# Layer norm's inverse deviation: from a column of sums and a trip through DRAM to products with a constant square

## The chip, the cores and the metric

The kernel runs on one NeuronCore of a Trainium2 chip. The metric is the device time of one execution in microseconds (us). TensorE (PE) multiplies matrices and writes to PSUM, which has 8 banks of 128 x 512 numbers of 4 bytes here. VectorE (DVE) and ScalarE (ACT) work elementwise on SBUF and PSUM, GpSimd (POOL) here mostly issues transfers that add, and SyncE (SP) issues the other transfers. Each engine works off its own list of instructions in order, and the engines wait for each other through semaphores. PEld is the loading of weights into TensorE's array, which overlaps with its products.

## The reference

One decoder layer on x of 1024 tokens by 1024 channels, in float32. The part that the change touches is the layer norm of the conv group, over the 1024 channels of each token:

```python
u = h @ w_in[l]
cv, cg, cs, lx, ls = jnp.split(u, [...], axis=-1)
v = cv * jax.nn.sigmoid(cg)
v = causal_depthwise_conv(v, dw_w[l], dw_b[l])        # 31 taps
v = jax.nn.silu(layernorm(v, cln_g[l], cln_b[l]))
v = v @ pw2_w[l] + pw2_b[l]
y_conv = v * jax.nn.silu(cs)
...
y = jnp.concatenate([y_conv, y_lru], axis=-1) @ w_out[l]
x = x + (1.0 + gate[:, None, :]) * y

def layernorm(x, g, b):
    mu = jnp.mean(xf, axis=-1, keepdims=True)
    var = jnp.mean(jnp.square(xf - mu), axis=-1, keepdims=True)
    y = (xf - mu) * lax.rsqrt(var + EPS)
```

## The kernel before

Channels lie on the partitions and tokens along the free axis: a matrix of 1024 channels by 1024 tokens is KT = 8 tiles of 128 x 1024, and a half (H) is 512 tokens. To keep float32 accuracy, each operand of a product is split into a high and a low part in fp32r (a cast on ScalarE, a subtraction on VectorE), and a product is three: high by high, high by low, low by high. `weights` loads a row of weights as raw, and makes whi (ScalarE, L336) and wlo (VectorE, L363) from it; `mm_k` (L494) emits the three products of 128 x 512 for one tile of the contraction. A row of output takes 8 x 3 products for each half, 48 in all. Their result is called ps, one bank for each half (ps_0, ps_1).

The stages follow each other on TensorE: the products with W_in, the gates of the recurrence, then the 8 rows of the lru half of W_out (m = 0 to 7, operands yh and yl, in the slots ("lru", m)), then the pointwise projection pw2 and the conv half of W_out, both in pairs of rows with seven products in place of eight (`quarters`, `pair_weights`, `pair_products`, L605: results pa, pb, pu, pc). For each lru row VectorE adds the result to x (acc, a SCALAR_TENSOR_TENSOR, L355), and acc goes to DRAM.

Layer norm lies beside the lru rows. `conv_sum` adds the eight tiles c of the convolution into csum; `layer_norm` splits csum into meanh and meanl and multiplies both by a constant square of 1/1024 (ones_r), so that each token's mean stands on every partition (L1262). VectorE subtracts it from each c, ScalarE squares, and VectorE sums the squares over the eight tiles into lnss (128 x 1024). What remains is a sum over the 128 partitions, then the root, then the reciprocal spread to all partitions. `spread_by_dma` does that: eight products with lnss as weights and one column of ones as the moving operand give the sums as a column, 128 tokens on the partitions by 8 (L1234, in plain float32); ScalarE takes the root with eps_t as bias, VectorE the reciprocal, a product with the identity turns it to 8 x 128 (L1238), ScalarE copies that into a piece of V, one transfer writes it to DRAM (lnrowd), and a second reads it back to all 128 partitions (lnbc). VectorE multiplies every c by lnbc, ScalarE applies Silu with the channel's gain and bias, and `quarters` makes the operands of pw2 from c: vha, vla, vhb, vlb, vhc, vlc, vhT, vlT.

The order of the instructions is set by a planner (`Plan`). Each operation has an engine, an estimated cost, a priority (lower goes first), and the buffers that it reads and writes. `Plan.order` runs through time: whenever an engine is free it takes, among the operations whose operands are ready and whose buffers fit in their pools, the one with the lowest priority; an activation whose table isn't loaded counts 2.0 more. Priority −1 in the steps of the root puts them ahead of nearly all else that is ready. What comes out is a fixed list for each engine; on the chip only the semaphores decide when an entry starts.

Of the kernel before, what the change touches and what calls it, by code (L numbers as in the profile page):

```python
# [9 lines left out]
F32 = mybir.dt.float32  # L10
F32R = mybir.dt.float32r
AF = mybir.ActivationFunctionType
ALU = mybir.AluOpType

P = 128
D = 1024
T = 1024
KT = D // P
H = 512
TAPS = 31  # L20
STAPS = 4
EPS = 1e-6
# [5 lines left out]
DWW = SCW + KT * STAPS  # L28
# [59 lines left out]
LOADS = "s0 a0 w0 s1 b0 w1 x1 W2 s2 x2 s3 x3 W4 s4 x4 s5 x5 W6 s6 x6 s7 x7 h0 h1 h2 h3 h4 h5 h6 h7".split()  # L88

SETS = {AF.Sigmoid: "sigmoid", AF.Silu: "silu", AF.Exp: "exp", AF.Tanh: "exp",  # L90
        AF.Sqrt: "sqrt"}


class Buf:
# [199 lines left out]
def hymba_layer(ctx: ExitStack, tc: tile.TileContext, xT, vecs, mod_w, w_first, w_in,  # L294
# [3 lines left out]
    act, dve, pool, pe, sp = nc.scalar, nc.vector, nc.gpsimd, nc.tensor, nc.sync  # L298

    const = ctx.enter_context(tc.tile_pool(name="const", bufs=1))  # L300
# [5 lines left out]
    dram = ctx.enter_context(tc.tile_pool(name="dram", bufs=1, space=bass.MemoryType.DRAM))  # L306
# [11 lines left out]
    S = Plan(pools)  # L318
# [11 lines left out]
    def ACT(prio, out, in_, func, n=T, bias=None, scale=None, accum=None, r=(), w=(),  # L330
            reserve=0, after=()):
        kw = {}

        def emit():
            if func == "copy":
                act.copy(out(), in_())  # L336
                return
            if bias is not None:
                kw["bias"] = bias
            if scale is not None:  # L340
                kw["scale"] = scale
            if accum is not None:
                kw["accum_out"] = accum
            act.activation(out=out(), in_=in_(), func=func, **kw)  # L344
        ptr = sum(x is not None and not isinstance(x, float) for x in (bias, scale))
        return S.op("ACT", a_cost(n, ptr) + (0.1 if accum is not None else 0), emit, prio, r, w,
                    table=SETS.get(func), reserve=reserve, after=after)
# [5 lines left out]
    def STT(prio, out, in0, scalar, in1, op0, op1, n=T, accum=None, r=(), w=(), after=()):  # L353
        def emit():
            dve.scalar_tensor_tensor(out=out(), in0=in0(), scalar=scalar, in1=in1(), op0=op0,  # L355
                                     op1=op1, accum_out=accum)
        return S.op("DVE", d_cost(n, not isinstance(scalar, float)), emit, prio, r, w,
                    lock=not in_psum(r), after=after)

    def TT(prio, eng, out, a, b, op, n=T, r=(), w=(), reserve=0, after=()):  # L360
        e = dve if eng == "DVE" else pool
        return S.op(eng, d_cost(n) if eng == "DVE" else p_cost(n),
                    lambda: e.tensor_tensor(out=out(), in0=a(), in1=b(), op=op), prio, r, w,  # L363
                    reserve=reserve, lock=not in_psum(r), after=after)
# [6 lines left out]
    def SUB(prio, eng, lo, full, hi, n=T, r=(), w=(), reserve=0):  # L371
        return TT(prio, eng, lo, full, lambda: hi().bitcast(F32), ALU.subtract, n, r, w, reserve)
# [8 lines left out]
    def DMA(prio, out, in_, nbytes, r=(), w=(), after=(), reserve=0):  # L381
        return S.op("SP", max(0.1, nbytes / 360e3),
                    lambda: sp.dma_start(out(), in_()), prio, r, w, after=after,
                    reserve=reserve)
# [7 lines left out]
    def big_buf(name, dt=F32, parts=1):  # L392
        return S.buf("big", name, dt, parts)

    def bank(name):
        return S.buf("bank", name)
# [5 lines left out]
    def part(b, a, e):  # L402
        if isinstance(b, Two):
            z = a // H
            return part(b.b[z], a - z * H, e - z * H)
        return lambda: b()[:, a:e]

    def halves(b, a, e):
        if isinstance(b, Two):
            return [(b.b[z], 0) for z in (0, 1) if z * H < e and a < z * H + H]  # L410
        return [(b, i) for i in range(b.parts) if i * (T // b.parts) < e
                and a < (i + 1) * (T // b.parts)]

    FULL_BYTES = P * T * 4


    V = const.tile([P, NVEC], F32, tag="V", name="V")
# [6 lines left out]
    ident = const.tile([P, P], F32, tag="ident", name="ident")  # L424
    make_identity(nc, ident)
    ones = const.tile([P, P], F32, tag="ones", name="ones")
    dve.memset(ones, 1.0)
    ones_r = const.tile([P, P], F32R, tag="ones_r", name="ones_r")
    dve.tensor_scalar(out=ones_r, in0=ones, scalar1=1.0 / D, scalar2=None, op0=ALU.mult)
    eps_t = const.tile([P, 1], F32, tag="eps", name="eps_t")  # L430
    dve.memset(eps_t, EPS)

# [73 lines left out]
    FULL = ((0, H), (H, T))  # L506
# [280 lines left out]
    for i, ld in enumerate(LOADS):  # L787
        p = due[ld] = i - 100.0
# [5 lines left out]
        elif ld[0] in "wW":  # L794
            nk = 1 + (ld[0] == "W")
            rw, hi, lo = fw[k - k % 2]
            n, o, js = nk * FW, (k % 2) * FW, range(k % 2, k % 2 + nk)
            keys = lambda b: [(b, j) for j in js]
            DMA(p, part(rw, o, o + n), lambda k=k, n=nk: w_first[:, k:k + n, :], n * P * 4,
                w=keys(rw))  # L800
            for j in range(k, k + nk):
# [4 lines left out]
                if j:  # L806
                    SUB(p, "DVE", fw_part(lo, j), fw_part(rw, j), fw_part(hi, j), FW,
                        r=[(rw, jj), (hi, jj)], w=[(lo, jj)])
# [35 lines left out]
    for k in range(KT):  # L844
        p = due[f"s{k}"]
# [3 lines left out]
        else:  # L849
            dot(SCALE[k], p - 1.5 * (k == 1), KT + k, [gs_op, *(split_u[:1] if k == 1 else [])])  # L850
        gs_op = S.op("DVE", 0.2, lambda k=k, a_=a_: dve.scalar_tensor_tensor(
            out=col(gs, k), in0=a_, scalar=col(b1, k), in1=vec("norm_g", k), op0=ALU.add,
            op1=ALU.mult), p, [("macc", KT + k), ("b1", 0)], [("gs", k)], lock=True)
        p = max(p, due[f"x{k}"] if k else p, due[f"w{k}"])
# [4 lines left out]
        for a, e in START if k < UK else ((0, T),):  # L859
            n = e - a  # L860
            hk = halves(x_, a, e)
            if k == 0 == a:
                o = TS(p, part(uh, a, e), part(x_, a, e), g, None, ALU.mult, n=n,
                       r=hk + [("gs", k)], w=halves(uh, a, e))
            else:
                o = ACT(p, part(uh, a, e), part(x_, a, e), AF.Copy, n, scale=g,
                        r=hk + [("gs", k)], w=halves(uh, a, e))
            if k == 0 == a:
                rw, hi, lo = fw[0]
                SUB(p, "DVE", fw_part(lo, 0), fw_part(rw, 0), fw_part(hi, 0), FW,  # L870
                    r=[(rw, 0), (hi, 0), *halves(uh, a, e)], w=[(lo, 0)])
# [3 lines left out]
                r=hk + halves(uh, a, e) + [("gs", k)], w=halves(ul, a, e)))  # L875
# [9 lines left out]
        for ch, (a, e) in enumerate(START):  # L885
            for i, ps in enumerate(psf):
                if (a, e) not in cuts[i] or k == 0 == a:
                    continue
                q = p + 0.1 * ch if k < LASTK else due[f"w{KT - 1}"] + 0.01 * ((i + 1) % 4) + 0.001 * ch
# [140 lines left out]
    v, c = {}, {}  # L1030
# [194 lines left out]
               w=[("gate1", i) for i in range(KT)])  # L1225


    def spread_by_dma(ss):
        pr, ps = -1, bank("lnss")
        sd, rs = S.buf("sd", "lnsd"), S.buf("rs", "lnrs")  # L1230

        def stats():
            for b in range(KT):
                pe.matmul(part(ps, b, b + 1)(), ss()[:, b * P:b * P + P], ones[:, 0:1],  # L1234
                          start=b == 0, stop=b == KT - 1, skip_group_check=True)

        def turn():
            pe.matmul(ps()[:KT, P:2 * P], rs()[:, :KT], ident, start=True, stop=True)  # L1238
        S.op("PE", 0.23 * KT, stats, pr, [ss], [ps], columns=4 * P * KT)
        ACT(pr, lambda: sd()[:, :KT], part(ps, 0, KT), AF.Sqrt, KT, bias=eps_t, scale=1.0 / D,  # L1240
            r=[ps], w=[sd])
        S.op("DVE", 0.2, lambda: dve.reciprocal(rs()[:, :KT], sd()[:, :KT]), pr, [sd], [rs])
        S.op("PE", 0.2, turn, pr, [rs], [ps], columns=4 * P)
        row, bc = V[:KT, DWW:DWW + P], big_buf("lnbc", parts=2)
        flat = dram.tile([KT, P], F32, tag="lnrow", name="lnrowd")
        ACT(pr, lambda: row, lambda: ps()[:KT, P:2 * P], "copy", P, r=[ps], w=[("V", 1)])
        DMA(pr, lambda: flat, lambda: row, KT * P * 4, r=[("V", 1)], w=[("lnrowd", 0)])
        DMA(pr, bc, lambda: flat.rearrange("b p -> (b p)").partition_broadcast(P), FULL_BYTES,
            r=[("lnrowd", 0)], w=[bc])
        return bc  # L1250

    def layer_norm():
        pr = 45
        mean = Two("mean")

        mh, ml = big_buf("meanh", F32R), big_buf("meanl", F32R)
        split(-1, mh, ml, csum)

        def mean_mm():
            for a, b in FULL:  # L1260
                for z, m in enumerate((mh, ml)):
                    pe.matmul(part(mean, a, b)(), ones_r, m()[:, a:b], start=z == 0, stop=z == 1)  # L1262
        S.op("PE", 0.91, mean_mm, -1, [mh, ml], mean.b)
        ss = big_buf("lnss")
        for t in range(KT):
            for a, b in FULL:
                TT(pr, "DVE", part(c[t], a, b), part(c[t], a, b), part(mean, a, b), ALU.subtract,
                   H, r=halves(c[t], a, b) + halves(mean, a, b), w=halves(c[t], a, b))
            if t == 0:
                ACT(pr, ss, c[t], AF.Square, r=[c[t]], w=[ss])  # L1270
            else:
                q = big_buf(f"lnsq{t}")
                ACT(pr, q, c[t], AF.Square, r=[c[t]], w=[q])
                TT(pr, "DVE", ss, ss, q, ALU.add, r=[ss, q], w=[ss])
        bc = spread_by_dma(ss)
        for t in range(KT):
            for a, b in FULL:
                TT(pr, "DVE", part(c[t], a, b), part(c[t], a, b), part(bc, a, b), ALU.mult, H,
                   r=halves(c[t], a, b) + halves(bc, a, b), w=halves(c[t], a, b))
            ACT(pr, c[t], c[t], AF.Silu, scale=vec("cln_g", t), bias=vec("cln_b", t), r=[c[t]],  # L1280
                w=[c[t]])

# [285 lines left out]
```

## Time and profile before

| | us |
|---|---|
| median of 3 runs (735.17 to 735.5) | 735.18 |
| the profiled execution | 735.33 |
| its span, from the first to the last instruction | 733.0 |
| PE busy | 723.8 (99%) |
| PEld busy | 601.9 (82%) |
| DVE busy | 636.8 (87%) |
| ACT busy | 458.6 (63%) |
| POOL busy | 98.0 (13%) |

The mean TensorE clock granted was 0.998. Times in the profile count from the start of the span; 2.33 us of the execution lie outside of it. A row of the list of instructions in time has the start, the duration, the engine, the line, the operation, result <- operands, the partitions x elements of both, and the count; in brackets stands the idle time of the engine just before and what ended it. A row of the chain has start, length, engine, result and line. In the list of waits the three numbers are the total, the count and the longest. Ends of products are modelled, so their starts are the better measure.

### The profile page before, as it was taken

The page shows a single profiled execution, that of the slowest core. Times are in us where ns is not written, and L with a number is a line of the kernel's source. Part 1 is how long each engine was busy: PE and PEld are TensorE (multiplying, and loading weights), DVE is VectorE, ACT ScalarE, POOL GpSimd, SP SyncE. Part 2 cuts the span into 40 slices and gives each one's busy share as a digit, 9 for nine tenths or more (in the row PEclk, how much of TensorE's full clock was granted, in tenths as well). Part 3 has the DMA queues.
Part 4 walks back from the last instruction along what each step waited for, and adds up shares of the span by engine and source line. Part 5 has one row for each costly group of instructions (what it writes and reads, how often), then busy time and mean ns, then how long its engine had stood idle before and what let it go on. Part 6 is the DMA issues. An engine that isn't in the chain of part 4 may idle for free.

```text
span 733.0 us, 8975 instructions
## 1 busy us (share of the span) xinstructions
PE 723.8 (99%) x3298; PEld 601.9 (82%) x3298; DVE 636.8 (87%) x907; ACT 458.6 (63%) x616; POOL 98.0 (13%) x107
## 2 busy tenths in 40 slices
PE   8999999999999999999999999999999999999996
PEld 7888888888888888888888888888888888887886
DVE  6999999899999987688899995997699757899647
ACT  6760585776877977957867896834564324656421
POOL 0034012031222332233121100000000000000001
PEclk9999999999999999999999999999999999999999
DMA  9952023388699699699884536343433430622306
GB/s 327 406 210 87 0 82 86 99 199 187 145 251 242 137 214 232 138 220 205 187 175 89 118 82 186 104 155 144 143 116 128 159 116 1 228 76 98 115 1 229
DMA packets 37498, 112.10 MB, mean 153 GB/s; under 512 B 4168, under 2 KB 12880, under 8 KB 37456
## 3 DMA queue, kind: packets, MB, share of 16 engines
q1 hardware_dynamic: 24064, 76.50, 29.4%
q0 software_dynamic: 12528, 34.26, 26.1%
q10 hardware_dynamic: 864, 0.79, 0.3%
q8 instruction: 25, 0.41, 0.2%
q14 instruction: 17, 0.14, 0.1%
HBM read 64.69 MB, written 12.59 MB: 105 GB/s over the span
## 4 chain that ended last, share of the span: by engine, by line
PE 96%; DVE 2%; DMA 1%; SPq 0%; ACT 0%; issue 0%; DVEq 0%
PE ps L494 65%; PE first L774 5%; PE pbpw L605 3%; PE pupw L605 3%; PE papw L605 3%; PE gate L1197 3%; PE puout L605 2%; PE paout L605 2%; PE out L675 2%; PE pcpw L605 1%; PE pb0out L605 1%; PE pcout L605 1%; DVE o L355 1%; DMA fraw<-in_w_first_dram 1%; PE late L774 1%; PE out6b L675 1%
## 5 line engine op out<-in xcount | busy, mean ns | idle before, releaser
L494 PE MATMUL ps<-uh,whi 128*128 128x512 f32 x576 | 224.2, 389 | 0.0
L494 PE MATMUL ps<-ul,whi 128*128 128x512 f32 x576 | 224.1, 389 | 0.0
L494 PE MATMUL ps<-uh,wlo 128*128 128x512 f32 x576 | 224.1, 389 | 0.0
L494 PEld LDWEIGHTS ps<-ul,whi 128*128 128x128 f32 x576 | 108.1, 188 | 22.5
L494 PEld LDWEIGHTS ps<-uh,whi 128*128 128x128 f32 x576 | 108.1, 188 | 22.5
L494 PEld LDWEIGHTS ps<-uh,wlo 128*128 128x128 f32 x576 | 108.1, 188 | 22.4
L336 ACT CAST whi<-raw 128x1024 fp32r<-128x1024 f32 x46 | 48.0, 1048 | 48.6 <-PE ps L494 39.0
L344 ACT ACT_TABLE_LOAD x48 | 61.6, 1283 | 6.2 <-DVE sp8h L377 3.1
L368 POOL DMA_DIRECT2D es<-cq x45 | 40.1, 904 | 164.5 <-ACT cq L344 130.1
L363 DVE TENSOR_TENSOR wlo<-raw,whi 128x1024 fp32r<-128x1024 f32 x39 | 47.5, 1219 | 14.8 <-ACT whi L336 14.5
L355 DVE SCALAR_TENSOR_TENSOR cacc<-v,V,cacc 128x511 f32<-128x511 f32 (+14 forms) x75 | 55.6, 741 | 0.5
L355 DVE SCALAR_TENSOR_TENSOR caccs<-v,V,caccs 128x511 f32<-128x511 f32 (+6 forms) x70 | 52.1, 744 | 1.3
L355 DVE SCALAR_TENSOR_TENSOR caccs<-c,wsum,caccs 128x511 f32<-128x511 f32 (+6 forms) x70 | 51.9, 742 | 0.5
L368 POOL DMA_DIRECT2D oo<-co x42 | 38.3, 913 | 89.3 <-ACT co L344 48.5
L494 PE MATMUL ps<-yh,whi 128*128 128x512 f32 x128 | 50.0, 391 | 0.0
L494 PE MATMUL ps<-yh,wlo 128*128 128x512 f32 x128 | 49.8, 389 | 0.0
L494 PE MATMUL ps<-yl,whi 128*128 128x512 f32 x128 | 49.8, 389 | 0.0
L363 POOL TENSOR_TENSOR o<-fin,bc 128x256 f32<-128x256 f32 x4 | 2.9, 730 | 284.1 <-DMA out_dram<-o 279.0
L355 DVE SCALAR_TENSOR_TENSOR xs<-ps,V,xs 128x512 f32<-128x512 f32 (+3 forms) x48 | 35.7, 744 | 0.2
L344 ACT ACTIVATE cq<-v,V 128x511 f32<-128x511 f32 (+14 forms) x45 | 31.9, 708 | 0.0
L355 DVE SCALAR_TENSOR_TENSOR modw<-modw,sc 128x1024 f32<-128x1024 f32 x23 | 30.1, 1312 | 0.0
L344 ACT ACTIVATE cq<-c,wsum 128x512 f32<-128x512 f32 x42 | 29.9, 714 | 0.0
(375 smaller groups left out, 1443.1 us busy)
## 6 DMA issues: line engine op xcount, KB each, us to landing
raw<-in_w_in_dram SPq DMA_DIRECT2D x36, 512.0 KB, 4.4
modw<-in_mod_w_dram SPq DMA_DIRECT2D x24, 512.0 KB, 9.0
raw<-in_w_out_dram SPq DMA_DIRECT2D x10, 512.0 KB, 3.8
scsd<-scs SPq DMA_DIRECT2D x8, 512.0 KB, 4.7
acc<-in_xT_dram SPq DMA_DIRECT2D x8, 512.0 KB, 4.4
accd<-acc SPq DMA_DIRECT2D x8, 512.0 KB, 2.7
rawpw<-in_pw_dram SPq DMA_DIRECT2D x8, 512.0 KB, 3.5
scsr<-scsd SPq DMA_DIRECT2D x8, 512.0 KB, 5.5
```

Source lines behind the costliest of these rows:

```text
L336: act.copy(out(), in_())
L344: act.activation(out=out(), in_=in_(), func=func, **kw)
L355: dve.scalar_tensor_tensor(out=out(), in0=in0(), scalar=scalar, in1=in1(), op0=op0, op1=op1, accum_out=accum)
L363: lambda: e.tensor_tensor(out=out(), in0=a(), in1=b(), op=op), prio, r, w,
L368: return S.op("POOL", ISSUE, lambda: pool.dma_start(out(), a(), accum_op=ALU.add), prio, r, w, lag=RATE * n / T, after=after)
L494: pe.matmul(part(ps, a - off, b - off)(), k3(lhs)()[:, k, :], rhs[k]()[:, a:b], start=(k == 0 and lhs is wh and rhs is xh and (a - off) % ...
L605: pe.matmul(part(ps, 0, c1 - c0)(), half(*lhs)()[:, j * P:j * P + P], half(*rhs)()[:, c0:c1], start=start and j == 0 and z == 0, stop=j == ...
L675: pe.matmul(part(ps, a - off, e - off)(), k3(lhs)()[:, k, :], rhs()[:, i * H + a % H:i * H + a % H + e - a], start=k == KORD[0] and lhs is ...
L774: pe.matmul(part(ps, a - off, b - off)(), fw_part(lhs, k, i * P, i * P + P)(), rhs()[:, a:b], start=k == 0 and lhs is wh and rhs is xh, st ...
L1197: pe.matmul(ps(), lhs()[:, j, :], rhs()[:, c0:c1], start=st == 0, stop=st == 2)
```

## The change

The trip through DRAM goes. In its place `root_by_ones` treats each half of 512 tokens by itself: ScalarE casts the half of lnss to fp32r (hi), VectorE subtracts to get lo, and TensorE multiplies both by a constant square, so that the sum over the partitions comes out on every partition at once. The square is now −1/1024 (minus_r, also used for the mean, whose subtraction becomes an addition); the bank holds minus the variance. ScalarE takes Abs_reciprocal_sqrt of it with scale −1 and bias eps_t, which gives a first y, and half its square (q). Two SCALAR_TENSOR_TENSORs on VectorE make one step of Newton's method, y · (1.5 − (var + eps) · y² / 2), into lnbc of that half. The multiplications of c then read the half's own lnbc.

```diff
-        AF.Sqrt: "sqrt"}
+        AF.Sqrt: "sqrt", AF.Abs_reciprocal_sqrt: "root"}
...
-    dve.tensor_scalar(out=ones_r, in0=ones, scalar1=1.0 / D, scalar2=None, op0=ALU.mult)
+    dve.tensor_scalar(out=minus_r, in0=ones, scalar1=-1.0 / D, scalar2=None, op0=ALU.mult)
...
-    def spread_by_dma(ss):
...
+    def root_by_ones(pr, ss, a, e, ps, out):
+        n, y, name = e - a, part(out, 0, e - a), f"{ss.name}{a}"
+        hi, lo, q = (big_buf(f"{z}{name}", d) for z, d in (("hi", F32R), ("lo", F32R), ("q", F32)))
+        neg, sk = part(ps, 0, n), halves(ss, a, e)
+        ACT(pr, part(hi, 0, n), part(ss, a, e), "copy", n, r=sk, w=[hi])
+        SUB(pr, "DVE", part(lo, 0, n), part(ss, a, e), part(hi, 0, n), n, r=[*sk, hi], w=[lo])
+
+        def total():
+            for i, m in enumerate((hi, lo)):
+                pe.matmul(neg(), minus_r, part(m, 0, n)(), start=i == 0, stop=i == 1)
+        S.op("PE", 2 * (n + 32) / 2400, total, pr, [hi, lo], [ps], columns=2 * n)
+        ACT(pr, y, neg, AF.Abs_reciprocal_sqrt, n, bias=eps_t, scale=-1.0, r=[ps], w=[out])
+        ACT(pr, part(q, 0, n), y, AF.Square, n, scale=0.5 ** 0.5, r=[out], w=[q])
+        STT(pr, neg, neg, -EPS, part(q, 0, n), ALU.add, ALU.mult, n, r=[ps, q], w=[ps])
+        STT(pr, y, neg, 1.5, y, ALU.add, ALU.mult, n, r=[ps, out], w=[out])
...
-                    pe.matmul(part(mean, a, b)(), ones_r, m()[:, a:b], start=z == 0, stop=z == 1)
+                    pe.matmul(part(mean, a, b)(), minus_r, m()[:, a:b], start=z == 0, stop=z == 1)
...
-        ss = big_buf("lnss")
+        ss = big_buf("lnss", parts=2)
...
-                TT(pr, "DVE", part(c[t], a, b), part(c[t], a, b), part(mean, a, b), ALU.subtract,
+                TT(pr, "DVE", part(c[t], a, b), part(c[t], a, b), part(mean, a, b), ALU.add,
...
-        bc = spread_by_dma(ss)
+        bc = [big_buf(f"lnbc{z}") for z in (0, 1)]
+        for z, (a, b) in enumerate(FULL):
+            root_by_ones(-1, ss, a, b, bank(f"lnss{z}"), bc[z])
         for t in range(KT):
-            for a, b in FULL:
-                TT(pr, "DVE", part(c[t], a, b), part(c[t], a, b), part(bc, a, b), ALU.mult, H,
-                   r=halves(c[t], a, b) + halves(bc, a, b), w=halves(c[t], a, b))
+            for z, (a, b) in enumerate(FULL):
+                TT(pr, "DVE", part(c[t], a, b), part(c[t], a, b), part(bc[z], 0, H), ALU.mult, H,
+                   r=halves(c[t], a, b) + [bc[z]], w=halves(c[t], a, b))
```

Since the planner works out the whole list anew, the diff doesn't show where things stand. The lists differ only from the sums of squares to the start of pw2; ahead of that and from the end of pw2's first pair on, every engine's order is the same. In the names below, numbers tell buffers of one name apart.

TensorE before, where the sums stand among the products of lru row 3, first half; the turn follows 12 products later:

```order
L494 MATMUL ps_0_4151<-yh_3883,whi_4076 128x512
L494 MATMUL ps_0_4151<-yl_3900,whi_4076 128x512
L494 MATMUL ps_0_4151<-yh_3883,wlo_4090 128x512
L1234 MATMUL lnss<-ones,lnss 128x1 x8
L494 MATMUL ps_0_4151<-yh_3893,whi_4076 128x512
L494 MATMUL ps_0_4151<-yl_3911,whi_4076 128x512
```

TensorE now, at the same row of W_out:

```order
L494 MATMUL ps_0_4150<-yh_3892,wlo_4089 128x512
L494 MATMUL ps_0_4150<-yh_3897,whi_4075 128x512
L494 MATMUL ps_0_4150<-yl_3922,whi_4075 128x512
L494 MATMUL ps_0_4150<-yh_3897,wlo_4089 128x512
L1237 MATMUL lnss_4188<-hilnss_4172,minus_r 128x512
L1237 MATMUL lnss_4188<-lolnss_4179,minus_r 128x512
L1237 MATMUL lnss_4191<-hilnss_4174,minus_r 128x512
L1237 MATMUL lnss_4191<-lolnss_4186,minus_r 128x512
L494 MATMUL ps_0_4150<-yh_3908,whi_4075 128x512
```

The four new products stand six main products later than the sums did, and six main products ahead of where the half row ends; the turn is gone.

VectorE before, from the last sum of squares to the first multiplications of c (lnsd and lnrs are the root and its reciprocal):

```order
L363 TENSOR_TENSOR lnss<-lnss,lnsq_4149 128x1024
L363 TENSOR_TENSOR wlo_4168<-raw_4010,whi_4156 128x1024
L1242 RECIPROCAL lnrs<-lnsd 128x8
L355 SCALAR_TENSOR_TENSOR acc_3995<-ps_0_4151,gate_92,acc_3995 128x512
L355 SCALAR_TENSOR_TENSOR acc_3995<-ps_1_4201,gate_92,acc_3995 128x512
L363 TENSOR_TENSOR c_970<-c_970,lnbc 128x512
L363 TENSOR_TENSOR wlo_4248<-raw_4100,whi_4235 128x1024
```

VectorE now:

```order
L363 TENSOR_TENSOR lnss<-lnss,lnsq_4148 128x1024
L363 TENSOR_TENSOR wlo_4167<-raw_4009,whi_4155 128x1024
L363 TENSOR_TENSOR lolnss_4179<-lnss,hilnss_4172 128x512
L363 TENSOR_TENSOR lolnss_4186<-lnss,hilnss_4174 128x512
L355 SCALAR_TENSOR_TENSOR acc_3994<-ps_0_4150,gate_92,acc_3994 128x512
L355 SCALAR_TENSOR_TENSOR lnss_4188<-lnss_4188,qlnss_4212 128x512
L355 SCALAR_TENSOR_TENSOR lnss_4191<-lnss_4191,qlnss_4217 128x512
L355 SCALAR_TENSOR_TENSOR lnbc_4194<-lnss_4188,lnbc_4194 128x512
L355 SCALAR_TENSOR_TENSOR lnbc_4207<-lnss_4191,lnbc_4207 128x512
L363 TENSOR_TENSOR c_969<-c_969,lnbc_4194 128x512
```

Six half-size instructions have taken the place of the reciprocal, the first acc stands in their middle, and the multiplications of c begin ahead of the second acc; the next wlo moves behind eight of them.

ScalarE before, in the same place:

```order
L336 CAST whi_4156<-raw_4010 128x1024
L344 ACT_TABLE_LOAD
L344 ACTIVATE lnsd<-lnss,eps_t 128x8
L336 COPY V<-lnss 8x128
L336 CAST whi_4235<-raw_4100 128x1024
L344 ACT_TABLE_LOAD
L344 ACTIVATE c_970<-c_970,V 128x1024
```

ScalarE now:

```order
L336 CAST whi_4155<-raw_4009 128x1024
L336 CAST hilnss_4172<-lnss 128x512
L336 CAST hilnss_4174<-lnss 128x512
L344 ACT_TABLE_LOAD
L344 ACTIVATE lnbc_4194<-lnss_4188,eps_t 128x512
L344 ACTIVATE lnbc_4207<-lnss_4191,eps_t 128x512
L344 ACTIVATE qlnss_4212<-lnbc_4194 128x512
L344 ACTIVATE qlnss_4217<-lnbc_4207 128x512
L344 ACT_TABLE_LOAD
L344 ACTIVATE c_969<-c_969,V 128x1024
L336 CAST whi_4262<-raw_4099 128x1024
```

The number of table loads is the same, 2; the first now stands behind two casts of lnss, and the next whi has moved behind the first Silu.

More of the change, by code (lines that the diff above doesn't have):

```diff
@@ L427, in hymba_layer @@
     dve.memset(ones, 1.0)
-    ones_r = const.tile([P, P], F32R, tag="ones_r", name="ones_r")
-    dve.tensor_scalar(out=ones_r, in0=ones, scalar1=1.0 / D, scalar2=None, op0=ALU.mult)
+    minus_r = const.tile([P, P], F32R, tag="minus_r", name="minus_r")
+    dve.tensor_scalar(out=minus_r, in0=ones, scalar1=-1.0 / D, scalar2=None, op0=ALU.mult)
     eps_t = const.tile([P, 1], F32, tag="eps", name="eps_t")
@@ L1225, in gate_mod @@
                w=[("gate1", i) for i in range(KT)])
-    def spread_by_dma(ss):
[L1229 to L1250, printed above, removed]
+    def root_by_ones(pr, ss, a, e, ps, out):
[12 more added lines that the diff above has]
+        STT(pr, y, neg, 1.5, y, ALU.add, ALU.mult, n, r=[ps, out], w=[out])
     def layer_norm():
```

## The prediction

> **What bounds the kernel now.** I read the head of the page and its chain first, then the stages around the change, then TensorE's own waits.
>
> ```profile
> span 733.0 us, 8975 instructions
> PE 723.8 (99%) x3298; PEld 601.9 (82%) x3298; DVE 636.8 (87%) x907; ACT 458.6 (63%) x616; POOL 98.0 (13%) x107
> ...
> PE 96%; DVE 2%; DMA 1%; SPq 0%; ACT 0%; issue 0%; DVEq 0%
> ```
>
> The chain that ended last runs through TensorE for 96% of the span. By stretch (PE, PEld, DVE, ACT, POOL busy, each with its count, then clock and DMA):
>
> ```profile
> 508.00:520.00 12.00, 12.00 (x62) 9.78 (x61) 2.70 (x4) 1.92 (x4) 0.00 (x0) 1.00 0.48 162
> 520.00:562.00 42.00, 42.00 (x187) 34.75 (x187) 42.00 (x61) 29.13 (x33) 0.00 (x0) 1.00 0.29 106
> 562.00:580.00 18.00, 18.00 (x81) 14.92 (x80) 17.53 (x24) 7.80 (x11) 0.00 (x0) 1.00 0.49 163
> ```
>
> TensorE has no gap from 508 to 580. VectorE is idle 12.00 − 2.70 = 9.3 us in 508 to 520, where layer norm waits, and then has not a moment free until 562. What TensorE waited for in the whole span:
>
> ```profile
> PE token_stats L740 <- DVE ones L427: 1.1, 1, 1.1
> PE puout L605 <- ACT eout L336: 0.7, 1, 0.7
> PE first L774 <- DVE ul L355: 0.6, 1, 0.6
> PE c_row L744 <- ACT cs L344: 0.4, 1, 0.4
> PE finbc L698 <- DVE finss L363: 0.2, 1, 0.2
> ```
>
> None of it belongs to layer norm. So the 12 us that the round trip through DRAM takes are covered by other products (L494), and to shorten that trip gains nothing by itself. What counts is how long the products of layer norm occupy TensorE, and whether any product waits that did not wait before.
>
> **The change part by part.** First, what leaves TensorE: the 16 passes of the sums (L1234) and the 2 of the turn (L1238). The chain gives them 1.68 + 0.32 = 2.00 us:
>
> ```profile
> 484.73 0.91 PE mean L1262 x4
> 485.64 23.12 PE ps L494 x102
> 508.76 1.68 PE lnss L1234 x16
> ...
> 513.32 0.32 PE lnss L1238 x2
> ...
> 562.83 2.72 PE papw L605 x12
> ```
>
> The same rows give the pace of the main products: 23.12 / 102 = 0.2267 us from start to start. I don't take the 2.00, because the starts show more:
>
> ```profile
> 508.37 0.39 PE L494 MATMUL ps<-yh,wlo 128*128 128x512 f32 x1
> 508.60 1.84 PE L1234 MATMUL lnss<-ones,lnss 128*128 128x1 f32 x16
> 510.30 0.49 PE L494 MATMUL ps<-yh,whi 128*128 128x512 f32 x1
> 510.62 0.40 PE L494 MATMUL ps<-yl,whi 128*128 128x512 f32 x1
> ...
> 513.25 0.39 PE L1238 MATMUL lnss<-ident,lnrs 128*8 128x128 f32 x2
> ...
> 515.52 0.39 PE L494 MATMUL ps<-yh,wlo 128*128 128x512 f32 x1
> ```
>
> ```profile
> 510.25:515.50 5.25, 4.96 (x20) 1.00 0.26 93
> ```
>
> The second fence counts L494's products that start between the sums and 515.52: 20. Without the sums and the turn, these 20 would have taken 20 × 0.2267 = 4.53 us from 508.60 on; they took 515.52 − 508.60 = 6.92. So sums and turn cost 2.39 us, 0.39 more than their own time: the first product behind them is followed 0.32 later (510.30 to 510.62) instead of 0.23, and those after it are a little slow. All of that leaves with them: −2.39.
>
> What comes to TensorE: 4 products of 128x512 with the constant square (high and low part of each half). The nearest row is the mean's four, of the same shape and kind with the same square: 0.91 us in the chain, and 102 products at 0.2267 follow at once, so they disturb nothing behind them. +0.91.
>
> TensorE's net: −2.39 + 0.91 = −1.48 us. Its bounds: with the chain's 2.00 in place of 2.39 it is −1.09; below −1.48 no row gives anything.
>
> The Trainium skill ("TensorE: Matmul & The Clock Gate", Back-to-back issue gap) puts a warm product of 512 columns at N/2.4 + 2.5 ns, 0.216 us. By it, as an estimate, the net would be −(6.92 − 20 × 0.216) + 4 × 0.216 = −1.74. The trace's 0.2267 over 102 products differs from the page, and I go by the trace.
>
> Second, whether the four products find their operands. VectorE, ScalarE and the prices (the list of groups from 480 to 575; for the activation with a pointer bias the tile view, minimum/median/maximum in ns):
>
> ```profile
> 506.75 1.22 DVE L363 TENSOR_TENSOR lnss<-lnss,lnsq 128x1024 f32<-128x1024 f32 x1
> 507.88 1.22 DVE L363 TENSOR_TENSOR wlo<-raw,whi 128x1024 fp32r<-128x1024 f32 x1
> 510.77 0.20 DVE L1242 RECIPROCAL lnrs<-lnsd 128x8 f32<-128x8 f32 x1 [1.68 <-ACT lnsd L344]
> 513.36 0.75 DVE L355 SCALAR_TENSOR_TENSOR acc<-ps,gate,acc 128x512 f32<-128x512 f32 x1 [2.38 <-PE ps L494]
> 519.35 0.75 DVE L355 SCALAR_TENSOR_TENSOR acc<-ps,gate,acc 128x512 f32<-128x512 f32 x1 [5.24 <-PE ps L494]
> 520.02 0.68 DVE L363 TENSOR_TENSOR c<-c,lnbc 128x512 f32<-128x512 f32 x1
> ```
>
> ```profile
> 506.22 1.04 ACT L336 CAST whi<-raw 128x1024 fp32r<-128x1024 f32 x1
> 507.28 1.28 ACT L344 ACT_TABLE_LOAD   x1
> ```
>
> ```profile
> L336 ACT CAST vha<-c 128x512 fp32r<-128x512 f32 x4 | 2.2, 614 | 0.0
> ...
> L363 DVE TENSOR_TENSOR vla<-c,vha 128x512 fp32r<-128x512 f32 x4 | 2.6, 679 | 0.0
> ...
> L355 DVE SCALAR_TENSOR_TENSOR acc<-ps,gate,acc 128x512 f32<-128x512 f32 x15 | 11.1, 741 | 8.5 <-PE ps L494 8.5
> ```
>
> ```profile
> L344 ACT ACTIVATE scs<-next,bias x4: 707/710/712, 98.8 to 100.6; 128x512 f32<-128x512 f32 x4
> ```
>
> The sum of squares lands at 506.75 + 1.22 = 507.97. The two casts follow on ScalarE until 507.97 + 2 × 0.61 = 509.2. On VectorE the order leaves wlo ahead of the two subtractions; it ends at 509.10, and they at 509.8 and 510.5 with no overlap; in the list four of them fill 2.6 us, 0.65 apiece, so rather 510.4. TensorE's order puts six main products where the sums stood, so the four take their slots at 508.60 + 6 × 0.2267 = 509.96, 510.18, 510.41 and 510.64. The low half of the second comes 0.1 to 0.2 before it is used. I take no wait; the other end is both subtractions waiting for both casts, one behind the other, 509.2 + 2 × 0.68 = 510.6 plus a weight load that may have to follow: a wait of 0.2 to 0.3.
>
> Third, the rest of the chain, which covers itself if its end is early enough. The table load moves behind the casts, 509.2 to 510.5; the first pair of products is done at 510.18 + 0.39 = 510.6. Two roots and two squares, 0.71 each, end at 510.6 + 4 × 0.71 = 513.4. VectorE meanwhile does acc from the finished ps bank, whose last six products follow the four, ready at about 512.4, to 513.2. Then come four SCALAR_TENSOR_TENSORs at 0.75 from 513.4 to 516.4. So the first multiplication of c starts at about 516.4, where it was 520.02: 3.6 us sooner, though VectorE has 2 × 0.68 + 4 × 0.75 − 0.20 = 4.2 us more to do. That work lies in the 9.3 idle. TensorE asks for pw2's operands 1.48 sooner, so the multiplications have to start by 518.5; 2.1 us are spare. The table load to Silu behind the squares, 513.4 to 514.7, lies before c is ready. In ScalarE's list the cast of the next weights (whi) moves from ahead of that load to behind the first Silu, to about 519 to 520. Behind the turn TensorE still has half a row of W_out, 24 products, and a whole row, 48, whose weights are made: 72 × 0.2267 = 16.3 us from about 513.5. So these weights are needed near 528, and the cover holds.
>
> Fourth, the queue. SP loses two transfers that it issued in a row, and the acc load behind them moves up:
>
> ```profile
> 515.23 0.34 SPq L383 DMA_DIRECT2D lnbc<-lnrowd  x1
> 515.75 0.33 SPq L383 DMA_DIRECT2D acc<-in_xT_dram  x1
> ```
>
> Nobody on TensorE waits for that load, so I give it nothing. Left out for the same reason: the constant's sign, and the subtraction of the mean that becomes an addition.
>
> Sum: 735.33 (the profiled execution, span 733.0) − 1.48 = 733.85. The median shown, 735.18, is 0.15 below that execution, so 733.70.
>
> **The rivals.** (a) The low halves come late, and TensorE waits 0.2 to 0.3: 733.95. For it: a spare of 0.1 to 0.2 only. Against it: the subtractions are taken here without overlap.
>
> (b) The slow pace behind the sums isn't theirs, and only 1.09 is gained: 734.1. Against it: 102 even starts before, and the pace is even again from 515.52.
>
> (c) The gain is given back at a later hand-over. The only wait after layer norm in TensorE's main run is at 664:
>
> ```profile
> 662.79 0.72 PE puout L605 x3
> ...
> 663.53 0.59 ACT eout L336
> ...
> 664.17 3.03 PE puout L605 x12
> ```
>
> If ScalarE's copy had its own clock, the wait would grow by what TensorE gains: 735.2. But the copy starts 0.02 after the product before it ends, so it comes sooner as well.
>
> (d) The other side: VectorE becomes the bound. It has no idle from 520 to 562, so whatever delays the first multiplication beyond 518.5 reaches pw2 almost one for one. Were the root's table load not hidden and each of the four activations twice 0.71, the squares would end at 511.0 + 1.28 + 4 × 1.42 = 518.0 and the multiplications start at 521.0: 2.5 us late, 736.2. The point from which it decides is 518.5 for a loss of the gain, 518.5 + 1.48 + 1.47 = 521.5 for slower by 0.2%, taken without any spare at pw2. The case for it, beside the 42.00 of 42.00: the Trainium skill ("Perfetto Trace Analysis", Identifying the Most-Contended Engine) judges TensorE by the share of weight loads and VectorE by its occupancy. By that rule VectorE, at 87% against 82%, would be the engine to spare, and the change adds to it. Against it: in the stretch that takes the additions VectorE is the emptier one, 2.70 of 12.00.
>
> **How the numbers follow.** Full gain: 0.60. (a) 0.18, (b) 0.08, (c) 0.08, (d) 0.06. About 0.2%, 1.47 us, is what a measurement of this kernel can tell from no change; faster by that is below 733.71. The likeliest case, 733.70, lies on that line: of its 0.60 I give 0.44 to faster and 0.16 to same, since small waits can only raise it. (a) to (c) are the same: 0.34, but for 0.02 of (a). So faster 0.46, same 0.48, slower 0.06. The range: full gain with 0.3 of scatter below, from 733.4; (a) and (b) with 0.4 above, to 734.5. That holds 0.86 and leaves (c) and (d) out.
>
> **What would show it.** Right: lnss products about 0.23 apart at 509.96 to 510.64 with 0.23 on either side, the first c by lnbc near 516, pw2's first product at 562.83 − 1.48, no TensorE wait between 500 and 660. A gap ahead of the second or fourth lnss product is (a); a wait at papw, pbpw or pupw for VectorE is (d); a longer wait at eout is (c); a pace above 0.23 from 508.6 on is (b). I am wrong in the mechanism if TensorE is even throughout and the time is still above 734.5.

## Result

| | before | after | ratio, 95% interval |
|---|---|---|---|
| first comparison, median of 12 runs each | 735.65 us | 733.58 us | 0.9972 [0.9963, 0.9981] |
| again, 32 and 11 runs | 735.15 us | 733.71 us | 0.9978 [0.9969, 0.9986] |
| a third time, 26 and 8 runs | 735.32 us | 733.62 us | 0.9975 [0.9965, 0.9985] |

By the medians the changed kernel is faster by 1.4 to 2.1 us. The prediction had 733.7 us, by a gain of 1.48.

The page's head, after:

```profile
span 731.4 us, 8952 instructions
...
PE 722.9 (99%) x3284; PEld 601.5 (82%) x3284; DVE 640.4 (88%) x912; ACT 461.3 (63%) x620; POOL 98.0 (13%) x107
```

TensorE has 14 instructions fewer and is busy 0.9 us less by modelled ends; VectorE and ScalarE work more, by 3.6 and 2.7 us. The stretches around layer norm, with the columns of the prediction's table (PE, PEld, DVE, ACT, POOL busy, clock, DMA):

```profile
508.00:520.00 12.00, 12.00 (x54) 9.95 (x53) 9.37 (x16) 8.95 (x11) 0.00 (x0) 1.00 0.36 138
520.00:562.00 42.00, 42.00 (x187) 34.76 (x186) 41.98 (x60) 25.76 (x31) 0.00 (x0) 1.00 0.27 97
```

VectorE's busy time in the first stretch rose from 2.70 to 9.37: the new work, and multiplications of c that begin earlier. TensorE is full in both stretches, as before. Its waits:

```profile
PE token_stats L740 <- DVE ones L427: 1.1, 1, 1.1
PE puout L605 <- ACT eout L336: 0.7, 1, 0.7
```

None is layer norm's, and none is new. The chain, from the mean to pw2, and at the hand-over to eout:

```profile
484.38 0.91 PE mean L1254 x4
...
509.77 0.91 PE lnss L1237 x4
510.67 50.32 PE ps L494 x222
560.99 2.72 PE papw L605 x12
...
661.69 0.59 ACT eout L336
...
662.33 3.01 PE puout L605 x12
```

From the mean's first product to papw's first is the stretch in which the kernels differ: 562.83 − 484.73 = 78.10 us before, 560.99 − 484.38 = 76.61 after. That is 1.49 less. The four new products start 0.2267 apart, without a gap ahead of or behind them, as the list in time shows:

```profile
509.38 0.39 PE L494 MATMUL ps<-yh,wlo 128*128 128x512 f32 x1
509.60 0.39 PE L1237 MATMUL lnss<-hilnss,minus_r 128*128 128x512 f32 x1
...
510.28 0.39 PE L1237 MATMUL lnss<-lolnss,minus_r 128*128 128x512 f32 x1
510.51 0.39 PE L494 MATMUL ps<-yh,whi 128*128 128x512 f32 x1
```

The steps on VectorE and ScalarE beside them:

```profile
508.66 1.28 DVE L363 TENSOR_TENSOR lolnss<-lnss,hilnss 128x512 fp32r<-128x512 f32 x2
...
512.74 1.29 DVE L355 SCALAR_TENSOR_TENSOR lnss<-lnss,qlnss 128x512 f32<-128x512 f32 x2
...
515.13 1.88 DVE L363 TENSOR_TENSOR c<-c,lnbc 128x512 f32<-128x512 f32 x3
```

```profile
510.26 1.27 ACT L344 ACTIVATE lnbc<-lnss,eps_t 128x512 f32<-128x512 f32 x2 [0.17 <-PE lnss L1237]
511.41 1.15 ACT L344 ACTIVATE qlnss<-lnbc 128x512 f32<-128x512 f32 x2
```

This execution began 0.35 us sooner than the one shown of before (484.38 against 484.73). So 515.13 here is 515.48 on the clock of the profile before, where the first multiplication of c stood at 520.02.

### The profile page after: what moved, and what is told of

Its sections match the earlier page's. It is cut to its first block, busy times and chain, and to the rows that moved or that the text cites. A ratio compares the mean times of both kernels' runs of the same rounds, so it can differ in the third digit from the quotient of the medians.

```text
span 731.4 us, 8952 instructions
## 1 busy us (share of the span) xinstructions
PE 722.9 (99%) x3284; PEld 601.5 (82%) x3284; DVE 640.4 (88%) x912; ACT 461.3 (63%) x620; POOL 98.0 (13%) x107
## 4 chain that ended last, share of the span: by engine, by line
PE 96%; DVE 2%; DMA 1%; SPq 0%; ACT 0%; issue 0%; DVEq 0%
PE ps L494 65%; PE first L774 5%; PE pbpw L605 3%; PE papw L605 3%; PE gate L1197 3%; PE pupw L605 3%; PE puout L605 2%; PE paout L605 2%; PE out L675 2%; PE pcpw L605 1%; PE pb0out L605 1%; PE pcout L605 1%; DVE o L355 1%; DMA fraw<-in_w_first_dram 1%; PE late L774 1%; PE out6b L675 1%
```

## Experiments

The theory: the time follows what TensorE is occupied with, because everything else of layer norm is covered. The rivals: the trip's length, VectorE's additions, or something outside layer norm counted. All times are beside runs of the kernel before on the same chip. For the profiles I compare the same stretch each time, from the mean's first product to papw's first: 78.10 before.

### The changed kernel as it is, twice more

> The changed kernel as it is. Theory (TensorE's occupancy counts): 1.48 us less than the kernel before, ratio 0.9980, and in the profile the stretch from the mean's first product to papw's first product is 78.10 - 1.48 = 76.62 us. Rival (something outside layer norm became faster too): about 2.1 us less, ratio 0.9972, as in the first comparison; then a stretch other than this one must be shorter in every profile of the changed kernel than in that of the kernel before.

> The changed kernel as it is, on the same chip as the two others: 1.48 us below the kernel before, ratio 0.9980. The stretch from the mean's first product to papw's first is 76.62 us; whatever the whole time differs from that of the other executions must lie ahead of the main products at 87 us.

Measured: 733.71 us, ratio 0.9978 [0.9969, 0.9986], and 733.62 us, ratio 0.9975 [0.9965, 0.9985]. The first of the two, its chain:

```profile
485.00 0.91 PE mean L1254 x4
...
561.62 2.72 PE papw L605 x12
...
637.78 5.44 PE out L675 x24
```

The stretch is 76.62 us, to the hundredth what the theory says; in the other execution it is 561.13 − 484.52 = 76.61. What differs from execution to execution lies, in these profiles, at the beginning. Here is the row of the first products in the chain, in the earliest and in the latest of all profiles (the first profile after, and the kernel with fourteen additions on VectorE, below):

```profile
13.12 30.50 PE first L774 x132
```

```profile
14.14 30.54 PE first L774 x132
```

In all thirteen profiles these products start between 13.12 and 14.14; and from the main products at 87 us to the mean's first product it is 397.25 us in every one that has the same list there. The first comparison's 2.07 us is therefore taken to be the 1.49 and scatter; its interval reaches down to 1.4 us, and the runs of before in it left no trace, so this isn't shown. The mean of 79 spans of the kernel before, from the runs beside all experiments, is 733.33; that of 31 spans of the changed kernel, from its three comparisons, 731.86. The difference is 1.47. Outside of the span the kernel before had 1.94 us on average (1.74 to 2.97), the changed one 1.79 (1.74 to 1.86). No view shows what these 0.15 us are; they stay open.

### The four products twice

```diff
         def total():
-            for i, m in enumerate((hi, lo)):
-                pe.matmul(...)
+            for _ in range(2):
+                for i, m in enumerate((hi, lo)):
+                    pe.matmul(...)
```

> The changed kernel with the four products with the constant square issued twice (the second four overwrite the first; nothing else moves). Theory (each product lengthens the end by what it occupies TensorE): 4 x 0.2267 = 0.91 us over the changed kernel, so 0.57 below the kernel before if that one is 1.48 below. The root comes 0.9 us later, which the spare behind it must take. Rival (products put in front of a covered chain are covered too): no difference from the changed kernel.

Measured: 734.72 us, ratio 0.9995 [0.9986, 1.0003], 1.01 above the changed kernel on the same chip.

```profile
484.90 0.91 PE mean L1255 x4
...
510.29 1.81 PE lnss L1238 x8
...
562.42 2.72 PE papw L605 x12
```

The stretch is 77.52, 0.90 longer than 76.62. A product added there costs its full slot, though the chain behind it is covered. That confirms the prediction's +0.91.

### The sums put back, and the turn put back

Both add dead work to the changed kernel, in front of the four products, whose first overwrites it.

```diff
         def total():
+            for b in range(KT if a == 0 else 0):
+                pe.matmul(part(ps, b, b + 1)(), ss()[:, b * P:b * P + P], ones[:, 0:1],
+                          start=b == 0, stop=b == KT - 1, skip_group_check=True)
...
```

> The changed kernel with the 16 passes of the removed sums put back as dead work in front of the four products (their 8 columns are overwritten at once). Theory (the sums cost more than their own time): 1.68 + 0.39 = 2.07 us over the changed kernel, and in the trace one step of about 0.32 and then steps above 0.2267 behind the sums. Rival (b), that the slow pace behind the sums was not theirs: 1.68 us, and 0.2267 from product to product at once. Against the kernel before that is +0.6 or +0.2 if the changed kernel is 1.48 below. The first multiplication of c comes 1.7 to 2.1 us later, at about 517, inside the spare.

Measured: 735.55 us, ratio 1.0007 [0.9998, 1.0015], 1.84 above the changed kernel.

```profile
484.95 0.91 PE mean L1257 x4
...
510.34 1.68 PE lnss L1237 x16
512.01 1.05 PE lnss L1240 x4
513.07 50.34 PE ps L494 x222
563.41 2.72 PE papw L605 x12
```

The stretch is 78.46, 1.84 longer. Neither number that I had written was right. The sums do cost more than their 1.68: the four products behind them take 1.05 in place of 0.91, and the next some 0.02 more. So rival (b) falls. But it is 0.16 and not 0.39. My expectation had put on the sums what the chain of before already divides: 2.89 − 12 × 0.2267 = 0.17 behind the sums and 49.19 − 216 × 0.2267 = 0.22 behind the turn. The next run tests the second part:

```diff
         def total():
+            if a == 0:
+                pe.matmul(ps()[:KT, P:2 * P], ones[:, :KT], ident, start=True, stop=True)
...
```

> The changed kernel with the turn's two passes put back as dead work in front of the four products (8 columns of ones as weights, the identity as the other operand; overwritten at once). The chain of the kernel before gives the turn 0.32 of its own and 49.19 - 216 x 0.2267 = 0.22 behind it. Theory (both belong to the turn, as the sums have 1.68 + 0.17 in the run with the sums): from the mean's first product to papw's first 76.62 + 0.54 = 77.16 us. Rival (the 0.22 was something else at that place): 76.94.

Measured: 734.28 us, ratio 0.9983 [0.9974, 0.9991], 0.66 above the changed kernel on its chip.

```profile
484.91 0.91 PE mean L1256 x4
...
510.30 0.32 PE lnss L1237 x2
510.61 1.13 PE lnss L1239 x4
511.74 50.33 PE ps L494 x222
562.07 2.72 PE papw L605 x12
```

The stretch is 77.16, 0.54 longer: 0.32 of the turn's own and, as the chain divides it, 0.22 in the four products behind it. Sums and turn together are 1.84 + 0.54 = 2.38, where the prediction has 2.39.

### The first multiplication of c made late

Seven and fourteen more multiplications on VectorE, in front of the first Newton step, write an unused half of q.

```diff
...
+            for _ in range(7 if a == 0 else 0):
+                dve.tensor_tensor(out=q()[:, H:], in0=q()[:, :H], in1=q()[:, :H], op=ALU.mult)
...
```

> The changed kernel with seven more VectorE multiplications of 128x512 (into an unused half of q) in front of the first Newton step: about 7 x 0.6 = 4.2 us, so the first multiplication of c starts at about 515.1 + 4.2 = 519.3. By the prediction's limit (518.5, less the 0.36 by which this execution began sooner: 518.2) 1.1 us of that reach pw2's products: 1.1 us over the changed kernel, with a wait of TensorE at papw or pbpw. Rival (VectorE, full from 520 to 562, has no spare, so what is put ahead comes out behind): 3.7 to 4.2 us over it. Rival (the cover is larger than I allowed): no difference.

> The changed kernel with fourteen such VectorE multiplications, about 8.4 us: the first multiplication of c starts at about 523.5. By the prediction's limit 5.3 us over the changed kernel; by the rival without spare 8 to 9 us over it; the slope between seven and fourteen is 4.2 us in both, so this run shows whether the loss is one for one once it has begun.

Measured: 736.4 us, ratio 1.0018 [1.0008, 1.0027], 2.69 above the changed kernel on the same chip; and 741.56 us, ratio 1.0088 [1.0074, 1.0102]. First the multiplications of c in the changed kernel (its first repeat; minimum/median/maximum in ns, first start and last end), then those of the kernel with seven, its chain, and its waits:

```profile
L363 DVE TENSOR_TENSOR c<-c,lnbc x16: 680/684/686, 515.8 to 527.9; 128x512 f32<-128x512 f32 x16
```

```profile
L363 DVE TENSOR_TENSOR c<-c,lnbc x16: 677/680/682, 520.9 to 532.4; 128x512 f32<-128x512 f32 x16
```

```profile
485.20 0.91 PE mean L1259 x4
...
512.90 0.75 DVE acc L355
...
571.78 0.73 PE pupw L605 x2
...
640.52 5.44 PE out L675 x24
```

```profile
PE pupw L605 <- DVE vlc L363: 1.0, 1, 1.0
...
PE pbpw L605 <- DVE l34pw L363: 0.3, 1, 0.3
```

And with fourteen, the multiplications, the chain and the longest wait:

```profile
L363 DVE TENSOR_TENSOR c<-c,lnbc x16: 679/682/684, 526.2 to 537.7; 128x512 f32<-128x512 f32 x16
```

```profile
485.39 0.91 PE mean L1259 x4
...
645.82 5.44 PE out L675 x24
```

```profile
PE ps L494 <- DVE wlo L363: 2.5, 1, 2.5
```

Counted from the mean's first product, the first multiplication comes 30.8 us later in the changed kernel, 35.7 with seven and 40.8 with fourteen: delays of 4.9 and 10.0. I had reckoned with 4.2 and 8.4, at 0.6 apiece; they stand 0.73 apart. The products `out` behind pw2 come 152.78, 155.32 and 160.43 after the mean: losses of 2.54 and 7.65. From seven to fourteen 5.1 more of delay give 5.1 more of loss, so between these two the loss is one for one. If it is so from its start, it begins after 4.9 − 2.54 = 2.4 us (10.0 − 7.65 gives the same). VectorE bounds the stage beyond that point: with seven, the chain that ended last runs through VectorE from 512.90 to 571.78.

Where TensorE waits is not the same in the two. With seven, papw's first product starts as long after the mean as in the changed kernel (561.65 − 485.20 = 76.45 us by the starts in the list in time, 561.45 − 485.00 = 76.45 there), and the whole loss falls in pw2's first pair, at pbpw and pupw. With fourteen, TensorE waits before pw2: in an lru row it waits 0.4 us for whi at 529.74 and 2.5 for wlo at 532.94, the weights that the planner moved behind the first Silu and behind eight multiplications of c. papw's first product starts at 566.86, 5.0 later after the mean than with seven, and pw2's first pair adds 2.6. Not all of the 5.0 is waiting. From 533 to 538 the granted clock was 0.66, and main products stood up to 0.43 apart in place of 0.2267. The wait for vlc, the last in the pair, ends 571.78 − 485.20 = 86.58 after the mean with seven and 577.05 − 485.39 = 91.66 with fourteen: 5.1 later, the same as the multiplications.

Neither expectation for seven was right. Of the difference between 1.1 and 2.54, about half is that the delay was longer than meant (4.9 in place of 4.2), and the rest is that the prediction's limit allowed a spare of 518.2 − 515.1 = 3.1 where it was 2.4. The 3.7 to 4.2 of the rival is wrong because there is a spare.

### The Newton step left out

```diff
-        ACT(pr, part(q, 0, n), y, AF.Square, n, scale=0.5 ** 0.5, r=[out], w=[q])
-        STT(pr, neg, neg, -EPS, part(q, 0, n), ALU.add, ALU.mult, n, r=[ps, q], w=[ps])
-        STT(pr, y, neg, 1.5, y, ALU.add, ALU.mult, n, r=[ps, out], w=[out])
...
```

> The changed kernel without the Newton step: no squares, none of the four SCALAR_TENSOR_TENSORs; the root of ScalarE is used as it comes. TensorE has the same products in the same order, VectorE 3 us and ScalarE 1.2 us less. Theory (that work lies in the idle time of VectorE): the same time as the changed kernel, within 0.2 us. Rival (VectorE bounds the stage from 520 to 562, so its additions cost): up to 3 us faster than the changed kernel.

Measured: 733.43 us, ratio 0.9979 [0.997, 0.9988], where the changed kernel had 0.9978 and 0.9975.

```profile
485.05 0.91 PE mean L1251 x4
...
561.67 2.72 PE papw L605 x12
```

The stretch is 76.62 again. The first multiplication of c comes at 513.4, 28.4 behind the mean in place of 30.8, and nothing is gained by it. So the Newton step costs no time in this kernel.

### The trip undone, TensorE given more

The kernel before, with the trip through DRAM replaced by products: the same kind of sums, root and reciprocal on a few columns, then eight plain f32 products with the identity that spread the row.

```diff
+    def spread_by_products(ss):
+        bc = big_buf("lnbc", parts=2)
+        for z, (a, e) in enumerate(FULL):
+            ps = bank(f"lnss{z}")
+            wk, _ = rstd(-1, [(ss, 0)], a, e, ps, z)
+            ACT(-1, part(bc, a, e), part(ps, 0, H), "copy", H, r=wk, w=halves(bc, a, e))
...
```

> The kernel before with only the trip through DRAM undone: the sums as before, their root and reciprocal, then eight plain f32 products of 128x128 with the identity that spread the row to all partitions, and a copy. The first multiplication of c comes sooner, as the two transfers are gone, but TensorE works more: 16 passes at 0.11 are about 1.8 us, less the turn's 0.32. Theory (only TensorE's occupancy counts): slower than the kernel before by 1.2 to 1.9 us. Rival (the trip's length counted): faster than the kernel before by up to 1.5 us.

Measured: 736.45 us, ratio 1.0017 [1.0008, 1.0026]: 1.31 slower than the kernel before.

```profile
484.87 0.91 PE mean L1246 x4
...
512.78 1.78 PE lnss L704 x16
514.57 49.68 PE ps L494 x219
564.25 2.72 PE papw L605 x12
```

```profile
L363 DVE TENSOR_TENSOR c<-c,lnbc x16: 681/683/692, 514.3 to 525.8; 128x512 f32<-128x512 f32 x16
```

The first multiplication of c comes at 514.3 in place of 520.0, and yet the stretch is 79.38, 1.28 longer. The spread adds 1.78 and 49.68 − 219 × 0.2267 = 0.03 behind it; the turn's 0.54 goes; the sum is 1.27. A layer norm that is 5.8 us sooner (29.4 behind the mean in place of 35.3) and occupies TensorE longer makes the kernel slower. That refutes the rival by which the trip's length counted.

### The low parts left out

```diff
-        SUB(pr, "DVE", part(lo, 0, n), part(ss, a, e), part(hi, 0, n), n, r=[*sk, hi], w=[lo])
...
-            for i, m in enumerate((hi, lo)):
-                pe.matmul(neg(), minus_r, part(m, 0, n)(), start=i == 0, stop=i == 1)
+            pe.matmul(neg(), minus_r, part(hi, 0, n)(), start=True, stop=True)
...
-        split(-1, mh, ml, csum)
+        ACT(-1, mh, csum, "copy", r=[csum], w=[mh])
...
```

> The changed kernel without the low parts of the mean's and of the squares' sums: 4 products of 128x512 fewer on TensorE (2 at the mean, 2 at the squares) and the subtractions that made the low parts. Theory: 4 x 0.2267 = 0.91 us below the changed kernel, 2.4 below the kernel before. Rival (the time is set elsewhere): no difference from the changed kernel.

> The changed kernel without the low parts of the mean's and of the squares' sums again, now beside the changed kernel on the same chip: 4 x 0.2267 = 0.91 us below it by the theory.

Measured: 732.96 us of 5 runs, ratio 0.9969 [0.9956, 0.9981]; and 733.47 us of 12, ratio 0.9976 [0.9967, 0.9985], beside 0.9975 [0.9965, 0.9985] of the changed kernel on the same chip. The chain of the second:

```profile
483.62 0.45 PE mean L1251 x2
...
560.69 2.72 PE papw L605 x12
```

The mean stands six main products earlier in this list, so the stretch is 77.07 − 6 × 0.2267 = 75.71 us, and 0.91 shorter than 76.62: in the profile the gain is there whole (the first run's profile has the same 560.17 − 483.10 = 77.07). The times don't show it on the one chip where both ran: 8 of the 12 runs lie between 732.7 and 733.7, four between 734.4 and 736.2, and of those four there is no trace. Whether this version is faster than the changed kernel is open, and it gives up the low bits of the mean and of the variance.

## Why the prediction was right

- **The bound and the removed products, −2.39.** Right. Put back one by one, the sums cost 1.84 and the turn 0.54. The 0.39 beyond their own 2.00 is theirs, 0.17 and 0.22, so rival (b) with its 734.1 is refuted.
- **The added products, +0.91.** Right: 0.91 in the chain, 0.90 when they were doubled. The stretch became 1.49 shorter against a predicted 1.48. By the 0.216 of the Trainium skill ("TensorE: Matmul & The Clock Gate", Back-to-back issue gap), which the page gives for an isolated product, the estimate was −1.74; the trace's 0.2267 gave the value that came.
- **The slots and the low halves, no wait.** Right. On the clock of before, the four started at 509.95 to 510.63 (509.60 to 510.28, and 0.35), predicted at 509.96 to 510.64. The second low half ended at 508.66 + 1.28 = 509.94 and was used at 510.28, 0.34 later where I had 0.1 to 0.2. Rival (a) did not come.
- **The first multiplication of c, 516.4.** It came at 515.48 on that clock, 0.9 sooner. The term that was mis-sized is the duration of operations of one kind behind each other: the two roots and two squares took 512.56 − 510.26 = 2.30 where I had 4 × 0.71 = 2.84, and the four SCALAR_TENSOR_TENSORs 515.13 − 512.74 = 2.39 where I had 4 × 0.75. In a row they start about 0.6 apart.
- **The limit of 518.5 and rival (d).** The mechanism is real, its point was 0.6 too late. The spare behind 515.8 was 2.4, so the limit is 518.2 in that execution, 517.9 on the clock of before. I had set 518.5 from the place of the first multiplication before, without knowing a spare there. With seven the waits came at pbpw and pupw, not at papw. With fourteen the longest came before pw2, for the lru weights that the prediction needs "near 528": TensorE was ready for them at 529.21 (528.98 + 0.2267), which is 528.55 on the clock of before, so that step was right too. With 515.48 the change kept clear of all this, the two misjudged times (516.4 and 518.5) did no harm, and VectorE's additions cost nothing, as the run without the Newton step shows. The Trainium skill ("Perfetto Trace Analysis", Identifying the Most-Contended Engine) would have VectorE spared, at 88% against 82% for weight loads; here VectorE did 3.6 us more without loss, and one product more on TensorE cost its full 0.2267.
- **The hand-over to eout, rival (c).** It moved along with the rest: from papw's first product to puout's x12 it is 664.17 − 562.83 = 101.34 before and 662.33 − 560.99 = 101.34 after.
- **The time.** 735.18 − 1.48 gave 733.70; the three medians are 733.58, 733.71 and 733.62. That the first comparison has 2.07 isn't explained by the stretch of layer norm, which is 1.48 to 1.49 shorter in each profile of the changed kernel. The chances were nearly even between faster and same, since the forecast lay on the line of 0.2%; the ratios 0.9972, 0.9978 and 0.9975 lie on the faster side of it, but each interval reaches across 0.998.

## What to carry to other kernels

Where one engine is full, price an edit by what it does to that engine's slots: a step that ended 5.8 us sooner was worth nothing and its products cost 1.28, while a Newton step on two other engines was free within their spare. Take the cost of a removed product from the starts around it, not from its own duration, since what follows it can be slow for a while. And find how far the cover reaches by making the covered step late on purpose, by two amounts: the difference shows the slope, and the rest the spare. Look in each at the place where the full engine waits, since a greater delay can strike somewhere else first.

## What was not expected of the hardware

- Plain f32 products cost more than their own passes. After 16 passes with one column, spaced 0.11, the four fp32r products that followed took 1.05 us in place of 0.91; after the turn's two passes they took 1.13. By the starts in the list in time, a part of the turn's excess lies ahead of it: it starts 0.32 after the product before it (509.91 to 510.23), in place of 0.2267. After the spread's 16 passes of 128 columns the chain puts only 0.03 behind them, but the starts show the same slow pace as behind the sums: eleven steps take 514.32 to 516.94, 2.62 in place of 11 × 0.2267 = 2.49, and the first is 0.31. What makes the products behind slow wasn't tried.
- In one run a wait of TensorE was followed by a lower clock, and cost more than its length. With fourteen additions, the products from 534.30 to 537.29, after the wait of 2.5 us, start 0.42 to 0.43 apart, and the granted clock from 533 to 538 is 0.66. With seven, whose longest wait there was 1.0, the clock stayed at 1.00 (572 to 600). How long a wait it takes wasn't tried.
- The same VectorE multiplication that writes the same half again and again starts every 0.73 us (5.1 for seven); multiplications of the same size into different tiles (c) start every 0.60 (three in 1.88, each 0.68). Which of the differences between them counts wasn't tried.
- Between the main products at 87 us and the mean the time is 397.25 us in every profile whose list is the same there. The first products start between 13.12 and 14.14. From there to the end of the span the changed kernel took 718.2 to 718.3 in each of its three profiles (731.4 − 13.12, 732.0 − 13.75, 731.5 − 13.27), so what differed between these lay at the beginning.
